# Delta rule: keys and values turned in the first stage, squares of the inversion through memory, one chunk ahead

## The chip, the cores and the metric

The kernel runs on one core of a Trainium2 chip. Its time is the device time of one execution in microseconds, the median of several runs. The core's engines are TensorE (PE, matrix products into PSUM), VectorE (DVE), ScalarE (ACT), GpSimd (POOL) and SyncE (SP, which here issues nearly all transfers). Each works through a queue of its own, in order; semaphores connect them.

## The reference

One inference step of a two-layer encoder for 2048 prompt tokens and 32 sample tokens, model width 1024, all in float32. The first layer is a gated delta rule with 8 heads of 128 channels:

```python
proj = x @ w_in                                   # q, k, v (3072 columns), z (1024), a, b (8 each)
qkv = silu(causal_conv(proj[..., :3072]))         # width 4, per channel
q = l2norm(q) * 128 ** -0.5;  k = l2norm(k)
# per head and token t, with decay g_t and strength beta_t:
#   S_t = exp(g_t) (I - beta_t k_t k_t^T) S_{t-1} + beta_t k_t v_t^T
#   o_t = S_t^T q_t
o = rmsnorm(o) * norm_w * silu(z)
x = layer_norm(alpha * x + o @ w_out)
```

It may be evaluated in blocks. With the Gram matrix of a block's keys, weighted by decay, as the strictly lower part of `tmat`, the block's updates come from solving `tmat u = v beta` and `tmat w = k beta exp(gcum)`; then the state goes from block to block. The second layer is attention over a window of two chunks with sinks, a gate and another layer norm; the change doesn't touch it.

## The kernel before, in words

Precise products are made by splitting each float32 operand into a high and a low part and adding three products (`project`, L79 to L81). The program has these stages.

**First stage** (`P1`). `w_in` has 32 row blocks of 128 channels: 8 heads of q (`i` = 0 to 7), of k (8 to 15), of v (16 to 23), then z. For each, TensorE multiplies five token blocks of 416, ScalarE copies them into a row `R` of 128 channels by all tokens, and `conv` makes the convolution and SiLU on ScalarE and VectorE: `y`, channels on partitions. `y` goes to memory by channel (scratch tensors `q`, `k`, `v`). For q and k, ScalarE squares it into the tile `th`, VectorE turns 32x32 blocks of the squares (L225) and sums over them (L226), which `norms` makes into lengths by token. From `i` = 16 on the order of work on all five engines is written out by hand (`ordered`): between the five blocks of one head stand the steps of the `conv` of the head before (a generator, advanced by `next(c)`), and the decay table E, chunk by chunk (`decays`). `th` has one buffer, `R` and `y` two.

**Gate** (`P1.z`, later `LateGate`): the products for z, 24 matmuls a block.

**Inversions ahead** (`Ahead`): beside the gate's products, the inverses of the first two chunks (the sample's 32 tokens, and the first 128 of the prompt).

**Delta stage** (`Delta`). 17 chunks: the sample's and 16 of 128 tokens. A pass `i` of the loop in `run` goes through the string `ORDER`; an entry such as `G0+2` means step G0 for chunk `i + 2`, and a digit 0 or 1 behind a name is a half of four heads. So one pass works on several chunks at different points. On TensorE, VectorE and ScalarE this order is the order of execution; SP's and POOL's queues are ordered by the planner of the language. The steps that matter:

- `Lk`, `Lq`, `Lv`, `Lz`, `LE`, `Lgb`: loads of a chunk's tiles. k has two buffers.
- `G`, `N` (L695, L702): Gram products of the keys in PSUM, times the decay table E, into the tile `npr` (two buffers).
- `NB`, `L` (L708, L717): ScalarE copies the four diagonal 32x32 blocks together, VectorE turns them so that a matrix entry stands by row and column for all heads: the squares.
- `TT`, `PC0` to `PC5`, `T1` to `T3` (`chain`, L729, L731): 31 steps of forward substitution on the squares, 25 of them (23 for the last five chunks) on POOL, the rest on VectorE.
- `SPR`, `U32`, `v1` to `v5` with the copies `y1`, `ta1`, `u1`, `ta2`, `u3`: the inverse of a 128 block out of those of 32.
- `tk`, `tv` (L818): TensorE turns k and v from channels to tokens, four heads a step; `kd`, `vn` (L825): ScalarE scales what it reads from PSUM into tiles.
- `gq`, `at`: products of keys and queries, times E. `ks`, `e`, `vp`, `vs`: what the state recalls, the error, the update. `os`, `oa`, `o`: outputs. `sp`, `SU`: the state's step.
- `sq`, `X`, `R`: norm of the outputs, with a root by Newton steps on VectorE (L484 to L495). `OSC` (L916): outputs times that root. `otr`, `z`, `st`: turned back by TensorE (L925), times the gate, stored.
- `GA0` to `GA3`, `gth`, `gz1`, `gz2`, `WH`, `WL`: the gate products still open, a quarter of a block each, with their VectorE and ScalarE steps. They end with pass 10; from pass 11 on `side` prepares the output projection.

PSUM banks of the pool `pa` (two) go to `G`, `tk`, `tv`, `gq`, v2 and v4.

After that follow the output projection, the second layer's projections and the attention.

Of the kernel before, what the change touches and what calls it, by code (L numbers as in the profile page):

```python
# [22 lines left out]
NP = 2048  # L23
# [74 lines left out]
class P1:  # L98
# [99 lines left out]
    def conv(self, i, R, parts):  # L198

        nc, T, one = self.nc, self.T, self.one  # L200
        kind, h = i // 8, i % 8
        nc.gpsimd.tensor_copy(self.convo[:, i, 0:3], R[:, NP:NP + 3])
        nc.gpsimd.tensor_copy(self.convo[:, i, 3:6], R[:, NT + 3:NT + 6])
        W = NT + 3
        y = self.big.tile([128, NT + 3], F32, tag="y", name="y")
        nc.scalar.activation(y[:], R[:, 0:W], AF.Copy, scale=self.convw[:, i, 0:1])  # L206
        for j in range(1, 4):
            yield
            nc.vector.scalar_tensor_tensor(out=y[:], in0=R[:, j:j + W], scalar=self.convw[:, i, j:j + 1], in1=y[:],  # L209
                                           op0=ALU.mult, op1=ALU.add)  # L210
# [7 lines left out]
        nc.sync.dma_start(dst[0:NTT - 1, :, h, :].rearrange("t p k -> p t k"),  # L218
                          y[:, 0:NP].rearrange("p (t k) -> p t k", k=128))
        (nc.sync if i >= self.FREE else nc.scalar).dma_start(dst[NTT - 1, :, h, 0:NS], y[:, NP + 3:NP + 3 + NS])  # L220
        if kind == 2:
            return
        nc.scalar.activation(th[:, 0:NP], y[:, 0:NP], AF.Square)
        nc.scalar.activation(th[:, NP:NT], y[:, NP + 3:NP + 3 + NS], AF.Square)
        nc.vector.transpose(R[:, 0:NT], th[:, 0:NT])  # L225
# [379 lines left out]
class Delta:  # L605
# [49 lines left out]
    def load(self, ch, name, halves=(0, 1)):  # L655
# [14 lines left out]
        else:  # L670
            for q in halves:
                if own:
                    t = ch.pool.tile([128, 4, w], F32, tag=f"c{name}{q}", name=name, bufs=1)[:]
                elif name == "q":
                    t = self.four.tile([128, 4, w], F32, tag="q", name="q", bufs=5)[:]
                else:
                    t = self.sml.tile([128, 4, w], F32, tag="vz", name=name, bufs=3)[:]
# [26 lines left out]
    def gather(self, ch):  # L704
        ch.nb = self.sml.tile([128, 8, 32], F32, tag="nb", name="nb")
        for b in range(ch.n // 32):
            bs = slice(32 * b, 32 * b + 32)
            self.nc.scalar.copy(ch.nb[bs], ch.npr[bs, :, bs])  # L708
# [5 lines left out]
    def turned(self, ch):  # L714
        n = ch.n
        ch.L = self.two.tile([128, 32, 32], F32, tag="L", name="L")
        self.nc.vector.transpose(ch.L[:n], ch.nb[:n].rearrange("q p i -> q i p").unsqueeze(2).to_broadcast([n, 32, 4, 8]))  # L717

    def chain(self, ch, P, a, z, tag):
# [6 lines left out]
        for j in range(a, z):  # L726
            i0, w = j + 1, j // 4 + 1
            sh = [n, 31 - j, w]
            P.tensor_tensor(out=tm[:n, i0 - k:, :w], in0=L[:n, i0:, j:j + 1].to_broadcast(sh),  # L729
# [85 lines left out]
    def turn(self, ch, x, name):  # L815
        tr = self.bank(self.pa, ch, name)
        for j in range(4):
            self.nc.tensor.transpose(tr[:ch.n, j, :], x[:, j, :ch.n], self.G["ident"][:, :])  # L818

    def scaled(self, ch, q, src, dst, table):  # L820
        n, tr = ch.n, ch.__dict__.pop(src + str(q))
        t = self.four.tile([128, 4, 128], F32, tag=dst, name=dst)
# [111 lines left out]
    def steps(self):  # L934
# [3 lines left out]
             "NB": self.gather, "TT": self.unit, "L": self.turned, "SPR1": self.spread, "SPR2": self.spread_back,  # L938
# [3 lines left out]
             "OSC": self.scale}  # L942
# [4 lines left out]
        for q in range(2):  # L947
# [6 lines left out]
            for name in "qvz":  # L954
                S[f"L{name}{q}"] = lambda c, name=name, q=q: self.load(c, name, (q,))
            S[f"tk{q}"] = lambda c, q=q: self.turn(c, c.k[:, self.heads(q)], f"ktr{q}")
            S[f"tv{q}"] = lambda c, q=q: self.turn(c, c.v[q], f"vtr{q}")
            S[f"kd{q}"] = lambda c, q=q: self.scaled(c, q, "ktr", "kd", "ekd")
            S[f"vn{q}"] = lambda c, q=q: self.scaled(c, q, "vtr", "vn", "hn")
# [9 lines left out]
    MADE = {"NB", "TT", "L", "T1", "T2", "T3", "PC0", "PC1", "PC2", "PC3", "PC4", "PC5"}  # L969
    HELD = {"Lgb", "Lk", "Lq0", "Lq1", "Lv0", "Lv1", "Lz0", "Lz1", "otr0", "otr1", "z0", "z1", "st0", "st1"}  # L970
    WORK = {"G0", "G1", "v1", "v2", "v3", "v4", "v5", "tk0", "tk1", "tv0", "tv1", "gq0", "gq1", "ks0", "ks1", "vp0", "vp1",
# [62 lines left out]
class Ahead(Delta):  # L1034
# [13 lines left out]
    def inverses(self, chunks):  # L1048
# [1367 lines left out]
def host_inputs(inp):  # L2416
# [116 lines left out]
```

## Time and profile before

| | |
|---|---|
| median of 3 runs | 2101.48 us (2099.33 to 2110.56) |
| profiled execution | 2110.58 us, span 2108.8 us |
| TensorE busy | 2048.6 us, 97%, granted clock 0.989 |
| VectorE, ScalarE, GpSimd busy | 1468.9 (70%), 989.0 (47%), 911.0 us (43%) |
| first stage | to about 605 us |
| inversions ahead, beside the gate | about 605 to 720 us |
| delta stage | about 720 to 1120 us |
| transferred | 360.85 MB, 171 GB/s over the span |

Rows of the timeline and of the chain that ended last start with the time from the span's start and the duration in us; then engine, line, operation and tiles. SPq rows are transfers as SP issues them. A bracket at the end of a row gives idle time before it and what released the engine. Rows of waits give the sum in us, the number of waits and the longest. TensorE's rows overlap, since matmuls are pipelined: its pace is read from start to start. A float32 product of 128x128 by 128x128 has two records, a transpose one.

### The profile page before, as it was taken

Reading aid. Unit: us, or ns where it says so; the run is one execution under the profiler, and the core shown is the slowest. Engines: PE = TensorE matmul, PEld = TensorE weight load, DVE = VectorE, ACT = ScalarE, POOL = GpSimd, SP = SyncE. Lnnn points to the kernel's source line nnn. Section 1 sums busy time; section 2 is a strip of 40 time slices with the busy share of each in tenths; the row PEclk is TensorE's granted clock in tenths of the full one; section 3 lists DMA queues with packets and bytes.
Section 4 is the critical chain, followed back from the end, with each engine's and each line's share of the span. In section 5 each row is a group of like instructions: output and inputs, shape, how many; then the busy total and the mean of one; then the engine's idle time right before and its main releaser. Section 6 shows DMA issues by size and latency. Waiting matters only on the chain.

```text
span 2108.8 us, 37301 instructions
## 1 busy us (share of the span) xinstructions
PE 2048.6 (97%) x13694; PEld 1875.4 (89%) x13694; DVE 1468.9 (70%) x2587; ACT 989.0 (47%) x2465; POOL 911.0 (43%) x1248
## 2 busy tenths in 40 slices
PE   7999999999999999999999999999999999999998
PEld 5999999999999999999887887889989997777775
DVE  4476666675647678888887887768877755566565
ACT  4354444446532267777762211534644445455552
POOL 0322223212222177778752112157436515566666
PEclk9999999999999999999999999999999999999999
DMA  5132333236665545455766666778776659533421
GB/s 206 33 90 88 97 110 111 82 102 226 193 185 179 182 137 179 159 169 182 271 209 227 212 213 219 254 229 296 243 240 222 226 171 317 127 101 107 114 72 66
DMA packets 292763, 360.85 MB, mean 171 GB/s; under 512 B 74260, under 2 KB 217460, under 8 KB 292564
## 3 DMA queue, kind: packets, MB, share of 16 engines
q1 hardware_dynamic: 278576, 334.29, 49.9%
q10 hardware_dynamic: 14004, 24.17, 3.6%
q8 instruction: 108, 1.77, 0.3%
q14 instruction: 75, 0.61, 0.1%
HBM read 235.54 MB, written 134.06 MB: 175 GB/s over the span
## 4 chain that ended last, share of the span: by engine, by line
PE 83%; DMA 7%; DVE 3%; POOL 3%; issue 2%; ACT 1%; SPq 0%; ACTq 0%; DVEq 0%; POOLq 0%
PE ps L79 12%; PE ps L81 11%; PE ps L80 11%; PE ot L1126 3%; PE ot L1127 3%; PE ot L1128 3%; PE S L1992 2%; PE po L1126 2%; PE ot L2025 2%; PE po L1128 2%; PE po L1127 2%; PE tr L2007 2%; PE X L1653 2%; PE X L1651 2%; PE X L1652 2%
## 5 line engine op out<-in xcount | busy, mean ns | idle before, releaser
L79 PE MATMUL ps<-act_hi,w_hi 128*128 128x416 f32 x1280 | 454.9, 355 | 0.0
L81 PE MATMUL ps<-act_hi,w_lo 128*128 128x416 f32 x1280 | 450.2, 352 | 0.0
L80 PE MATMUL ps<-act_lo,w_hi 128*128 128x416 f32 x1280 | 447.9, 350 | 0.0
L79 PEld LDWEIGHTS ps<-act_hi,w_hi 128*128 128x128 f32 x1280 | 240.3, 188 | 3.8 <-issue 0.4
L80 PEld LDWEIGHTS ps<-act_lo,w_hi 128*128 128x128 f32 x1280 | 240.6, 188 | 3.0
L81 PEld LDWEIGHTS ps<-act_hi,w_lo 128*128 128x128 f32 x1280 | 240.1, 188 | 3.3
L209 DVE SCALAR_TENSOR_TENSOR y<-R,convw,y 128x2083 f32<-128x2083 f32 x72 | 182.5, 2536 | 60.9 <-ACT y L206 44.9
L56 POOL TENSOR_TENSOR w_lo<-w_raw,w_hi 128x1024 fp32r<-128x1024 f32 x25 | 71.4, 2858 | 330.9 <-ACT w_hi L55 303.6
L729 POOL TENSOR_TENSOR tm<-L,Tt 128x60 f32<-128x60 f32 (+19 forms) x365 | 132.5, 363 | 84.8 <-issue 39.9
L1826 POOL TENSOR_TENSOR P<-e,sm 128x384 f32<-128x384 f32 (+2 forms) x128 | 102.3, 820 | 118.0 <-DVE sm L1816 111.6
L731 POOL TENSOR_TENSOR Tt<-Tt,tm 128x60 f32<-128x60 f32 (+19 forms) x365 | 139.8, 383 | 28.6
L1812 ACT ACTIVATE e<-S,nm 128x193 f32<-128x193 f32 (+2 forms) x260 | 104.6, 415 | 97.3 <-DVE nm L1807 56.5
L1330 DVE TENSOR_TENSOR w_lo<-w_raw,w_hi 128x512 fp32r<-128x512 f32 x132 | 136.7, 1053 | 18.5 <-ACT w_hi L1342 12.7
L1126 PE MATMUL po<-wo_hi,g_hi 128*128 128x512 f32 x256 | 104.9, 410 | 8.1 <-DVE r L1134 7.9
L305 ACT COPY R<-ps 128x416 f32<-128x416 f32 (+1 forms) x144 | 60.4, 442 | 109.3 <-PE ps L81 95.8
L1482 ACT ACTIVATE o<-X 128x416 f32<-128x416 f32 x80 | 41.4, 518 | 134.7 <-PE X L1653 134.6
L1126 PE MATMUL ot<-wo,g_hi 128*128 128x512 f32 x256 | 103.6, 405 | 0.0
L1128 PE MATMUL po<-wo_hi,g_lo 128*128 128x512 f32 x256 | 101.2, 396 | 0.5 <-DVE g_lo L1169 0.5
L1127 PE MATMUL po<-wo_lo,g_hi 128*128 128x512 f32 x256 | 101.1, 395 | 0.0
L1127 PE MATMUL ot<-wo,g_hi 128*128 128x512 f32 x256 | 100.8, 394 | 0.0
L1128 PE MATMUL ot<-wo,g_lo 128*128 128x512 f32 x256 | 100.8, 394 | 0.0
L1342 ACT CAST w_hi<-w_raw 128x512 fp32r<-128x512 f32 x129 | 76.8, 616 | 21.5 <-PE ps L1652 6.7
(362 smaller groups left out, 5119.4 us busy)
## 6 DMA issues: line engine op xcount, KB each, us to landing
w_raw<-in_b_w SPq DMA_DIRECT2D x60, 512.0 KB
w_raw<-in_w_in SPq DMA_DIRECT2D x40, 512.0 KB
act_raw<-s_hT SPq DMA_DIRECT2D x64, 208.0 KB
s_rows<-o SPq DMA_DIRECT2D x50, 208.0 KB
k<-s_k SPq DMA_DIRECT2D x17, 512.0 KB
E<-s_E SPq DMA_DIRECT2D x17, 512.0 KB
s_bq<-s_rows SPq DMA_DIRECT2D x40, 208.0 KB
s_bz<-o SPq DMA_DIRECT2D x40, 208.0 KB
```

Of the source, the lines that this page charges most:

```text
L79: nc.tensor.matmul(ps, hi[:, k, :], xh[:, k, :], start=(k == 0), stop=False)
L80: nc.tensor.matmul(ps, hi[:, k, :], xl[:, k, :], start=False, stop=False)
L81: nc.tensor.matmul(ps, lo[:, k, :], xh[:, k, :], start=False, stop=(k == KC - 1))
L209: nc.vector.scalar_tensor_tensor(out=y[:], in0=R[:, j:j + W], scalar=self.convw[:, i, j:j + 1], in1=y[:], op0=ALU.mult, op1=ALU.add)
L729: P.tensor_tensor(out=tm[:n, i0 - k:, :w], in0=L[:n, i0:, j:j + 1].to_broadcast(sh), in1=Tt[:n, j:j + 1, :w].to_broadcast(sh), op=ALU.mult)
L731: P.tensor_tensor(out=Tt[:n, i0:, :w], in0=Tt[:n, i0:, :w], in1=tm[:n, i0 - k:, :w], op=ALU.subtract)
L1126: nc.tensor.matmul(ps[:n], ghi[:, k, :n], hi, start=a, stop=False)
L1127: nc.tensor.matmul(ps[:n], ghi[:, k, :n], lo, start=False, stop=False)
L1128: nc.tensor.matmul(ps[:n], glo[:, k, :n], hi, start=False, stop=z)
L1330: P.tensor_tensor(out=lo, in0=raw, in1=hi, op=ALU.subtract)
L1812: self.nc.scalar.activation(x.e[:, h, u, :x.n], x.S[:, h, u, :], AF.Exp, bias=x.nm[:, h, u:u + 1], scale=1.0, accum_out=x.sm[:, h, u:u + 1])
L1826: self.nc.gpsimd.tensor_tensor(out=x.P[:, u, :nj * 128].rearrange("r (j h k) -> r j h k", h=2, k=64), in0=x.e[:, :, u, :n].rearrange("r h ...
```

## The change

Keys and values are turned to token order in the first stage and go to memory that way; k still goes by channel as well, and by token into the new scratch tensor `kt`. VectorE turns 32x32 blocks of `y` into `th`, and four pairs of transfers write 32 channels each: pieces of 32 floats, every 4 KB. For k, ScalarE squares the turned tile into `R`, and VectorE sums. In the delta stage one load of 512 KB each (`Lt`, `Lv`) brings kd and vn by token, and ScalarE scales them in place; the steps `tk` and `tv` are gone. The squares go from `npr` to memory (`WN`, four transfers of 32x32 blocks of all heads), and come back as four loads that read each head's square on the partitions that use it (`L`); `NB` and the VectorE transpose are gone, and `chain` reads the square by the other index. `G` and `N` are made one chunk earlier, at the end of a pass, and `Lk` stands in the middle.

```diff
@@ conv
-        dst = T["qkv"[kind]]
-        nc.sync.dma_start(...)                      # by channel, for q, k and v
-        if kind == 2:
-            return
-        nc.scalar.activation(th[:, 0:NP], y[:, 0:NP], AF.Square)
-        nc.vector.transpose(R[:, 0:NT], th[:, 0:NT])
+        if kind < 2:
+            dst = T["qk"[kind]]
+            nc.sync.dma_start(...)                  # by channel, for q and k
+        pieces = (th[:, 0:NP], y[:, 0:NP]), (th[:, NP:NT], y[:, NP + 3:NP + 3 + NS])
+        if kind == 0:
+            for a, b in pieces:
+                nc.scalar.activation(a, b, AF.Square)
+            nc.vector.transpose(R[:, 0:NT], th[:, 0:NT])
+        else:
+            for a, b in pieces:
+                nc.vector.transpose(a, b)
+            self.by_token(T[("kt", "v")[kind - 1]], h, th)
+            if kind == 2:
+                return
+            yield
+            nc.scalar.activation(R[:, 0:NT], th[:, 0:NT], AF.Square)
+    def by_token(self, dst, h, turned):
+        for a in range(4):
+            s = slice(32 * a, 32 * a + 32)
+            self.nc.sync.dma_start(dst[0:NTT - 1, :, h, s].rearrange("t (b i) j -> i (t b) j", i=32),
+                                   turned[s, 0:NP].rearrange("i (b j) -> i b j", j=32))
+            self.nc.sync.dma_start(dst[NTT - 1, 0:NS, h, s], turned[s, NP:NT])
@@ ordered
-                for _ in range((2, 2, 1, 1, 0)[b]):
+                for _ in range((2, 2, 1, 1, int(i == self.FREE + 1))[b]):
@@ Delta
     ORDER = """
-        ta2+0 fq1+1 os0+0 v5+0 Lk+2 PC2+1 OSC+-1 Lq1+2 PC3+1 fq0+1 vn0+1 G0+2 u3+0 N0+2 G1+2 TT+2 otr0+-1
-        otr1+-1 N1+2 GA1+1 z0+-1 NB+2 tk0+1 tk1+1 vp0+0 vs0+0 PC4+1 kd0+1 st0+-1 z1+-1 Lv1+1 GA3+0 fk+1 L+2
-        PC5+1 kd1+1 vp1+0 Lv0+2 st1+-1 T1+1 oa0+0 T2+1 sp0+0 T3+1 tv1+1 SPR1+1 PC0+2 LE+3 o0+0 vs1+0 SU0+0 gq1+2
-        PC1+2 SPR2+1 os1+0 sp1+0 vn1+1 Lz0+0 oa1+0 SU1+0 sq0+0 at1+2 v1+1 Lgb+2 WH+1 gq0+2 at0+2 o1+0 y1+1 ks0+1
-        e0+1 U32+1 ks1+1 v2+1 v3+1 GA2+1 gth+0 sq1+0 WL+1 X+0 Lz1+0 Lq0+3 ta1+1 v4+1 gz1+0 tv0+2 GA0+2 u1+1 e1+1
-        R+0 gz2+0
+        ta2+0 fq1+1 os0+0 v5+0 PC2+1 OSC+-1 Lq1+2 PC3+1 L+2 fq0+1 vn0+1 u3+0 TT+2 otr0+-1 otr1+-1
+        GA1+1 z0+-1 vp0+0 vs0+0 PC4+1 kd0+1 st0+-1 z1+-1 GA3+0 fk+1 PC5+1 kd1+1 vp1+0 st1+-1 T1+1
+        oa0+0 T2+1 sp0+0 T3+1 SPR1+1 PC0+2 LE+3 o0+0 vs1+0 SU0+0 gq1+2 PC1+2 SPR2+1 os1+0 sp1+0
+        vn1+1 Lz0+0 oa1+0 SU1+0 sq0+0 at1+2 v1+1 Lgb+2 Lt+2 WH+1 gq0+2 at0+2 o1+0 y1+1 ks0+1
+        e0+1 U32+1 ks1+1 Lk+3 v2+1 v3+1 GA2+1 gth+0 sq1+0 Lv+2 WL+1 X+0 Lz1+0 Lq0+3 ta1+1
+        v4+1 G0+3 gz1+0 GA0+2 u1+1 N0+3 G1+3 e1+1 R+0 N1+3 WN+3 gz2+0
+    def by_token(self, ch, src, dst):
+        t = self.two.tile([128, 8, 128], F32, tag=dst, name=dst)
+        ch.__dict__[dst] = t[:, 0:4], t[:, 4:8]
+        self.nc.sync.dma_start(t[:ch.n], self.T[src][ch.ti, :ch.n])
-    def gather(self, ch):
-        ch.nb = self.sml.tile([128, 8, 32], F32, tag="nb", name="nb")
+    def keep_squares(self, ch):
         for b in range(ch.n // 32):
             bs = slice(32 * b, 32 * b + 32)
-            self.nc.scalar.copy(ch.nb[bs], ch.npr[bs, :, bs])
+            self.nc.sync.dma_start(self.T["N"][ch.ti, b].rearrange("p j i -> j p i"), ch.npr[bs, :, bs])
-    def turned(self, ch):
+    def squares_back(self, ch):
         ch.L = self.two.tile([128, 32, 32], F32, tag="L", name="L")
-        self.nc.vector.transpose(ch.L[:n], ch.nb[:n].rearrange("q p i -> q i p").unsqueeze(2).to_broadcast([n, 32, 4, 8]))
+        for b in range(ch.n // 32):
+            src = self.T["N"][ch.ti, b].rearrange("p j i -> p (j i)").unsqueeze(0).to_broadcast([4, 8, 1024])
+            self.nc.sync.dma_start(ch.L[32 * b:32 * b + 32].rearrange("q j i -> q (j i)"), src)
@@ chain
-            P.tensor_tensor(out=tm[:n, i0 - k:, :w], in0=L[:n, i0:, j:j + 1].to_broadcast(sh),
+            P.tensor_tensor(out=tm[:n, i0 - k:, :w], in0=L[:n, j, i0:].unsqueeze(2).to_broadcast(sh),
@@ scaled: no tiles of its own, no PSUM
+        n, t = ch.n, ch.__dict__[name][q]
         for j in range(4):
             h = q * 4 + j
+            self.nc.scalar.activation(t[:n, j, :], t[:n, j, :], AF.Copy, scale=self.G[table][:n, ch.ti, h:h + 1])
@@ inverses (Ahead)
-            self.gather(tmp)
+            self.keep_squares(tmp)
             self.unit(tmp)
             yield
-            self.turned(tmp)
+            self.squares_back(tmp)
@@ SCRATCH
+    "kt": (NTT, 128, 8, 128),
+    "N": (NTT, 4, 8, 32, 32),
```

More of the change, by code (lines that the diff above doesn't have):

```diff
@@ L216, in conv @@
         yield
-        dst = T["qkv"[kind]]
-        nc.sync.dma_start(dst[0:NTT - 1, :, h, :].rearrange("t p k -> p t k"),
-                          y[:, 0:NP].rearrange("p (t k) -> p t k", k=128))
-        (nc.sync if i >= self.FREE else nc.scalar).dma_start(dst[NTT - 1, :, h, 0:NS], y[:, NP + 3:NP + 3 + NS])
-        if kind == 2:
-            return
-        nc.scalar.activation(th[:, 0:NP], y[:, 0:NP], AF.Square)
-        nc.scalar.activation(th[:, NP:NT], y[:, NP + 3:NP + 3 + NS], AF.Square)
-        nc.vector.transpose(R[:, 0:NT], th[:, 0:NT])
+        if kind < 2:
+            dst = T["qk"[kind]]
+            nc.sync.dma_start(dst[0:NTT - 1, :, h, :].rearrange("t p k -> p t k"),
+                              y[:, 0:NP].rearrange("p (t k) -> p t k", k=128))
+            (nc.sync if i >= self.FREE else nc.scalar).dma_start(dst[NTT - 1, :, h, 0:NS], y[:, NP + 3:NP + 3 + NS])
+        pieces = (th[:, 0:NP], y[:, 0:NP]), (th[:, NP:NT], y[:, NP + 3:NP + 3 + NS])
[11 more added lines that the diff above has]
+            nc.scalar.activation(R[:, 0:NT], th[:, 0:NT], AF.Square)
         nc.vector.tensor_reduce(out=parts[:, h, :], in_=R[:, 0:NT].rearrange("p (c j) -> p c j", j=32),
@@ L676, in load @@
                 else:
-                    t = self.sml.tile([128, 4, w], F32, tag="vz", name=name, bufs=3)[:]
+                    t = self.sml.tile([128, 4, w], F32, tag="z", name=name, bufs=3)[:]
                 ch.__dict__.setdefault(name, {})[q] = t
                 nc.sync.dma_start(t[:, :, :n], T[name][ti, :, q * 4:q * 4 + 4, :n])
+    def by_token(self, ch, src, dst):
+        t = self.two.tile([128, 8, 128], F32, tag=dst, name=dst)
+        ch.__dict__[dst] = t[:, 0:4], t[:, 4:8]
+        self.nc.sync.dma_start(t[:ch.n], self.T[src][ch.ti, :ch.n])
     @staticmethod
@@ L813, in join5_out, with scaled @@
             self.nc.scalar.mul(self.u[:64, ps, 64:128], ch.u2p[hv, ps], -1.0)
[L815 to L822, printed above, removed]
+    def scaled(self, ch, q, name, table):
+        n, t = ch.n, ch.__dict__[name][q]
         for j in range(4):
             h = q * 4 + j
-            self.nc.scalar.activation(t[:n, j, :], tr[:n, j, :], AF.Copy, scale=self.G[table][:n, ch.ti, h:h + 1])
-        ch.__dict__.setdefault(dst, {})[q] = t
+            self.nc.scalar.activation(t[:n, j, :], t[:n, j, :], AF.Copy, scale=self.G[table][:n, ch.ti, h:h + 1])
     def pairs(self, ch, q):
@@ L941, in steps @@
              "u3": self.join5_out, "fk": lambda c: self.fade(c, c.k, slice(0, 8)), "X": self.mean, "R": self.root,
-             "OSC": self.scale}
+             "OSC": self.scale, "Lt": lambda c: self.by_token(c, "kt", "kd"), "Lv": lambda c: self.by_token(c, "v", "vn")}
         for j in range(6):
@@ L953, in steps @@
                 S[f"{name}{q}"] = lambda c, f=f, q=q: f(c, q)
-            for name in "qvz":
+            for name in "qz":
                 S[f"L{name}{q}"] = lambda c, name=name, q=q: self.load(c, name, (q,))
[L956 to L959, printed above, removed]
+            S[f"kd{q}"] = lambda c, q=q: self.scaled(c, q, "kd", "ekd")
+            S[f"vn{q}"] = lambda c, q=q: self.scaled(c, q, "vn", "hn")
             S[f"fq{q}"] = lambda c, q=q: self.fade(c, c.q[q], self.heads(q))
@@ L968 @@
     INVERT = {"v1", "y1", "v2", "ta1", "v3", "u1", "v4", "ta2", "v5", "u3", "U32", "G0", "G1", "N0", "N1"}
-    MADE = {"NB", "TT", "L", "T1", "T2", "T3", "PC0", "PC1", "PC2", "PC3", "PC4", "PC5"}
-    HELD = {"Lgb", "Lk", "Lq0", "Lq1", "Lv0", "Lv1", "Lz0", "Lz1", "otr0", "otr1", "z0", "z1", "st0", "st1"}
-    WORK = {"G0", "G1", "v1", "v2", "v3", "v4", "v5", "tk0", "tk1", "tv0", "tv1", "gq0", "gq1", "ks0", "ks1", "vp0", "vp1",
+    MADE = {"WN", "TT", "L", "T1", "T2", "T3", "PC0", "PC1", "PC2", "PC3", "PC4", "PC5"}
+    HELD = {"Lgb", "Lk", "Lq0", "Lq1", "Lz0", "Lz1", "otr0", "otr1", "z0", "z1", "st0", "st1"}
+    WORK = {"G0", "G1", "v1", "v2", "v3", "v4", "v5", "gq0", "gq1", "ks0", "ks1", "vp0", "vp1",
             "os0", "os1", "oa0", "oa1", "sp0", "sp1", "otr0", "otr1"}
@@ L1057, in inverses @@
         yield
-        for name in ("gb", "q", "v"):
+        for name in ("gb", "q"):
             self.load(chunks[0], name)
```

3 lines of the change are left out of this document (1 added, 2 removed).

## The prediction

> **What bounds the kernel now.** I read the page's first table, then the stretches by time, the waits of the delta stage, and last the timelines of TensorE (PE) and VectorE (DVE) through one of its iterations.
>
> ```profile
> span 2108.8 us, 37301 instructions
> PE 2048.6 (97%) x13694; PEld 1875.4 (89%) x13694; DVE 1468.9 (70%) x2587; ACT 989.0 (47%) x2465; POOL 911.0 (43%) x1248
> ```
>
> ```profile
> core 0: us, PE busy (x) PEld busy (x) DVE busy (x) ACT busy (x) POOL busy (x), PEclk, DMA share, GB/s
> 500.00:550.00 50.00, 50.00 (x267) 49.54 (x266) 30.02 (x22) 32.22 (x71) 15.33 (x13) 1.00 0.71 221
> 760.00:860.00 100.00, 100.00 (x1137) 95.98 (x1136) 85.68 (x204) 70.59 (x227) 78.73 (x205) 1.00 0.50 163
> ```
>
> TensorE is full in the first stage (500 to 550 us) and in the delta stage (760 to 860), at full granted clock. In the delta stage each chunk of 128 tokens is one pass through `ORDER`, and the start of its Gram products G shows the pace in the chain that ended last:
>
> ```profile
> 761.97 1.98 PE g L695 x16
> 784.88 1.98 PE g L695 x16
> 951.39 1.98 PE g L695 x16
> ```
>
> From 784.88 to 951.39 are seven passes: 23.79 us each. The waits between 760 and 960 have no row for TensorE. POOL, which carries 25 of the 31 steps of each inversion, waits little:
>
> ```profile
> POOL tm L729 <- DVE tm L729: 12.0, 9, 1.6
> ```
>
> That is 1.33 us a pass: its own pace is 23.79 - 1.33 = 22.46. So two engines stand near the limit, and TensorE is a hair ahead. One pass on TensorE (start, duration):
>
> ```profile
> 856.17 2.05 PE L695 MATMUL g<-k 128*128 128x128 f32 x16
> 858.06 1.04 PE L925 MATMUL otr<-ident,o 128*128 128x128 f32 x8
> 860.07 1.03 PE L818 MATMUL ktr<-ident,k 128*128 128x128 f32 x8
> ...
> 865.64 0.60 PE L818 MATMUL vtr<-ident,v 128*128 128x128 f32 x4
> 866.97 1.06 PE L870 MATMUL op<-Sp,q 128*128 128x128 f32 x8
> 871.37 1.95 PE L846 MATMUL ks<-Sp,k 128*128 128x128 f32 x16
> 873.25 0.62 PE L779 MATMUL tp<-y,u 64*64 64x64 f32 x13
> ...
> 876.73 0.66 PE L818 MATMUL vtr<-ident,v 128*128 128x128 f32 x4
> 878.36 1.05 PE L870 MATMUL op<-Sp,q 128*128 128x128 f32 x8
> 879.35 0.68 PE L808 MATMUL u2p<-u,ta 64*64 64x64 f32 x16
> 879.96 0.38 PE L695 MATMUL g<-k 128*128 128x128 f32 x1
> ```
>
> and on VectorE, up to the multiplication OSC (L916) whose result `otr` turns back:
>
> ```profile
> 874.55 0.68 DVE L854 TENSOR_TENSOR vn<-vn,ks 128x512 f32<-128x512 f32 x1
> 875.14 0.17 DVE L484 TENSOR_SCALAR ro_y<-Xo 128x8 int32<-128x8 int32 x1
> ...
> 877.39 0.77 DVE L563 SCALAR_TENSOR_TENSOR z<-zth,z 128x416 f32<-128x416 f32 x1
> 878.09 0.82 DVE L841 TENSOR_TENSOR q<-q,gb 128x512 f32<-128x512 f32 x1
> 878.82 1.37 DVE L916 TENSOR_TENSOR o<-o,ro_y 128x1024 f32<-128x1024 f32 x1
> ```
>
> Both engines run their program order here: the rows follow `ORDER` step by step.
>
> **The change part by part.** *Transposes off TensorE.* Sixteen a chunk go (tk, tv). Sixteen products of G take 1.89 us by starts (856.17 to 858.06), and a transpose is one such record, so at most 0.12 each: 8 ktr and 4 vtr within the stretch 858.06 to 873.25 are 1.3 (taken as 0.87 + 0.44), all sixteen 1.74 us a pass, 17 chunks at most 30 us. This is worth that much only while TensorE sets the pace.
>
> *Turned writes in the first stage.* VectorE gets 8 large transposes for v; those for k take the place of the ones of the squares:
>
> ```profile
> L225 DVE STREAM_TRANSPOSE R<-th 128x2080 f32<-128x2080 f32 x16 | 37.5, 2341 | 37.8 <-ACT th L224 37.8
> L717 DVE STREAM_TRANSPOSE L<-nb 128x1024 f32<-128x1024 f32 (+1 forms) x17 | 34.4, 2022 | 1.7 <-ACT nb L708 1.7
> ```
>
> 8 x 2.34 = 19 us, under a TensorE that needs 120 matmuls x 50/267 = 22.5 us a head; in 500 to 550 VectorE is 60% busy and would be 70%. Cost 0; without that cover 19 us. SP gets eight issues a head in place of two for v, beside two for k. A megabyte of 512-byte rows holds SP as long as the short transfer behind it is stuck in its issue (min/median/max):
>
> ```profile
> L220 SPq DMA_DIRECT2D s_v<-y x8: 1596/3185/5999, 455.1 to 604.3; - x8
> ```
>
> The same megabyte in 128-byte pieces costs between the same 3.2 us (price by bytes) and 4 x 3.2 = 12.8 (by pieces). I take the middle, 8, since these writes are short pieces in many rows: behind them queue the weight fetch, the decay table's loads and the gate's stores, and the `th` tile stays taken. Both ends lie under 22.5 us, and six PSUM buffers let TensorE run on: 0, at either end.
>
> *Squares through memory.* Seventeen L717 (2.02 us) leave VectorE, and the copies of the diagonal blocks leave ScalarE; both engines had slack, so 0 in themselves. In their place come four small stores, a wait on them, and four loads a chunk on SP. kt adds 512 KB a chunk, the squares as much again; DMA was at 0.50.
>
> *Gram products one chunk ahead, at the end of a pass.* This is the part that decides. `G0+3` now stands behind v4, `N0+3` behind `gz1`, and ahead of `e1`, the root R and OSC on VectorE. That adds a wait: VectorE's N0 waits for G0, and behind N0 are queued e1, R, N1, gz2, fq1, OSC; TensorE's otr waits for OSC, and the rest of TensorE's pass waits behind otr. G0 itself waits for the k tile, whose buffer (two of them) comes free with `ks1` of the same pass. So a ring closes once a pass:
>
> N0 starts 0.92 after G0 (the rows below), then N0 0.69, e1 0.59 (874.55 to 875.14), R 2.25 (875.14 to 877.39), N1 0.69, gz2 0.70 and fq1 0.73 (to the next start each), OSC 1.37: 7.9, with the signal 8.0.
>
> ```profile
> 723.33 1.78 PE g L695 x16
> ```
>
> ```profile
> 724.25 0.69 DVE L702 TENSOR_TENSOR npr<-g,E 128x512 f32<-128x512 f32 x1 [0.79 <-PE g L695]
> ```
>
> otr to the end of ks1 on TensorE: 873.25 - 858.06 = 15.19, less the 1.3 of transposes: 13.9. Then the wait for k, at least the work in front of G0 (873.25 to 876.73: 3.48). The k loads after the gate's products have ended show their price, from the chain and from SP's issue to TensorE's start:
>
> ```profile
> 1011.67 6.43 DMA k<-s_k
> 1035.22 5.44 DMA k<-s_k
> ```
>
> ```profile
> 990.12 0.32 SPq L666 DMA_DIRECT2D k<-s_k  x1
> 1056.20 0.32 SPq L666 DMA_DIRECT2D k<-s_k  x1
> ```
>
> ```profile
> 994.75 1.46 PE L695 MATMUL g<-k 128*128 128x128 f32 x11 [0.36 <-DMA k<-s_k]
> 1060.39 2.05 PE L695 MATMUL g<-k 128*128 128x128 f32 x16
> ```
>
> 4.63, 6.43, 5.44, and at most 4.19 (no wait): mean 5.2, which I take; ends 3.48 and 6.43. Today G starts 6.7 us after ks1, so this load is hidden; that cover goes. A pass becomes 8.0 + 13.9 + 5.2 = 27.1 us against 23.79. Even with k at no cost it is 25.4: without the ring's wait TensorE would reach otr 0.95 (G0, half of 1.89) + 1.2 (GA0, 876.73 to 878.36 less four transposes) + 0.95 (G1) + 0.99 (os0, 878.36 to 879.35) + 0.61 (v5, to 879.96) = 4.7 us after G0's start, and OSC ends 8.0 after it.
>
> *Sum.* G of chunk 3 to G of chunk 16 (761.97 to 1060.39) is 298.4 us in 13 passes. After: nine full ones, 243.9; one without a gate product after otr (1.2 less), 25.9; one without two, 24.6; two without gz2 as well, 23.9 each: 342.2, or +44. Before chunk 3, three chunks lose their transposes (-5), while each of the two inversions done ahead waits for its squares (two landings, some 6 us; the second is in VectorE's way): 0 together. After chunk 16 there is no G left to wait for, and the squares' round trip stands in front of the last inversion: 0 to +5, taken as 0. So +44 on the profiled 2110.58, which is 2155; that run was 9 us above the median of the three, 2101.48, and on the median the sum is 2145.
>
> **The rivals.** *Faster: the late start of R does not reach TensorE.* Then the pace falls to POOL's 22.46: 9 x 1.33, and 4 x 1.74 where POOL has fewer steps: -19, 2082. It decides if OSC ends within 4.7 us of G0, 3.3 earlier than the rows say. For it speaks that VectorE loses 2.02 us a pass; against it, that none of the lost work lies between G0 and OSC. 12%.
>
> *k hidden.* If k lands within 3.48, passes are 25.4, 24.2, 22.9 and 22.2: 320, +22, 2123. For it: 4.19 at the most once. Against: the three others, and 1 MB more to move a pass. 12%.
>
> *The squares land late and POOL sets the pace.* N1 ends 5.1 after G0; four issues at 0.4 and a small store as below, four issues and a load like k's: they land 5.1 + 1.6 + 3.3 + 1.6 + 5.2 = 16.8 after G0.
>
> ```profile
> 994.92 3.31 DMA s_z<-z
> ```
>
> POOL then needs 22.46, the rest of the steps to ks1 some 7 to 9, k 5.2, in two passes: 25.7 to 26.7 each, just under the 27.1. Five us more in the loads give 28.2 to 29.2, some +1.6 x 11 on top: 2163. 8%. [...]
>
> *The token writes slow the first stage.* Should a 128-byte piece cost twice a 512-byte row, a head holds the queue 25.6 us against 22.5: 16 x 3.1, +50 on top, 2195. 5%. [...]
>
> **How the numbers follow.** The three runs span 0.53% of their median, so 0.5% (10.5 us) is about what tells from no change. The forecast has 63%: 2130 to 2163 by the ends of k. 2108 to 2172 takes in k hidden and the late squares, with 6 us either side for what the start and the tail hold: 83%. Faster 0.12; slower is the rest but for 0.07 in which k is hidden and the tail gains.
>
> **What would show it.** Right: G to G near 27 us; waits of G on `k<-s_k` and of otr on DVE o L916, some 1.7 and 3.3 us a pass; no PE wait before 600; POOL waiting several us a pass. Wrong: a gapless TensorE in the delta stage, G to G under 23.8, or PE waits in the first stage.

## The result, and the profile after

| | before | after |
|---|---|---|
| median (4 runs each, the same chip) | 2105.18 us (2099.33 to 2110.56) | 2237.14 us (2234.03 to 2240.17) |
| ratio, 95% interval | | 1.0628 (1.0605 to 1.0651) |
| profiled span | 2108.8 us | 2231.9 us |
| TensorE's granted clock | 0.989 | 0.96 |

The change makes the kernel 6.3% slower. The forecast was slower by 2%: the direction and the ring that it named hold, the size doesn't. The profiled executions are 123.1 us apart and the medians 132.0, since the profile before is of the slowest of its four runs and the one after of the fastest. The page of the changed kernel, first table:

```profile
span 2231.9 us, 37147 instructions
PE 2060.5 (92%) x13422; PEld 1888.1 (85%) x13422; DVE 1448.8 (65%) x2594; ACT 970.5 (43%) x2392; POOL 878.7 (39%) x1248
```

TensorE has fewer instructions and is busy for longer: some of them run slower, which the stretches by time explain (PEclk is the granted clock of the stretch):

```profile
core 0: us, PE busy (x) PEld busy (x) DVE busy (x) ACT busy (x) POOL busy (x), PEclk, DMA share, GB/s
425.00:450.00 25.00, 11.71 (x56) 11.22 (x56) 19.69 (x9) 8.81 (x10) 8.10 (x8) 0.73 0.60 129
700.00:750.00 50.00, 42.04 (x202) 39.88 (x201) 28.70 (x85) 9.87 (x19) 6.84 (x15) 0.86 0.66 203
760.00:860.00 100.00, 87.82 (x856) 82.05 (x856) 60.84 (x158) 52.78 (x169) 55.28 (x150) 0.90 0.55 167
```

The stretch 760 to 860 was full at clock 1.00 before. There are also holes at 425 to 450 (first stage) and 700 to 750 (start of the delta stage) that I had priced at nothing. The Gram products G mark the passes again, those of chunks 3, 12 and 16 in TensorE's timeline:

```profile
785.28 0.91 PE L718 MATMUL g<-k 128*128 128x128 f32 x6 [1.25 <-DMA k<-s_k]
1053.46 0.77 PE L718 MATMUL g<-k 128*128 128x128 f32 x2 [3.76 <-DMA k<-s_k]
1182.01 1.41 PE L718 MATMUL g<-k 128*128 128x128 f32 x5 [8.20 <-DMA k<-s_k]
```

Before, they started at 761.97, 973.97 and 1060.39 (the second one in its timeline:)

```profile
973.97 0.38 PE L695 MATMUL g<-k 128*128 128x128 f32 x1
```

So the 123.1 us of longer span divide like this:

| stretch | before | after | longer by | forecast |
|---|---|---|---|---|
| up to G of chunk 3 | 762.0 | 785.3 | 23.3 | 0 |
| nine passes to G of chunk 12 | 212.0 | 268.2 | 56.2 | 31.9 |
| four passes to G of chunk 16 | 86.4 | 128.6 | 42.1 | 11.9 |
| from there to the end | 1048.4 | 1049.9 | 1.5 | 0 |

Waits of TensorE between 780 and 1185, and one pass on TensorE:

```profile
PE g L718 <- DMA k<-s_k: 57.7, 13, 9.1
PE otr L945 <- DVE o L936: 26.8, 11, 3.4
```

```profile
872.48 2.05 PE L718 MATMUL g<-k 128*128 128x128 f32 x8 [3.47 <-DMA k<-s_k]
...
874.67 0.55 PE L80 MATMUL ps<-act_lo,w_hi 128*128 128x416 f32 x1
875.02 0.55 PE L81 MATMUL ps<-act_hi,w_lo 128*128 128x416 f32 x1
...
877.99 1.06 PE L890 MATMUL op<-Sp,q 128*128 128x128 f32 x8
...
881.47 1.94 PE L945 MATMUL otr<-ident,o 128*128 128x128 f32 x8 [1.81 <-DVE o L936]
...
883.55 0.55 PE L80 MATMUL ps<-act_lo,w_hi 128*128 128x416 f32 x1
883.90 0.55 PE L81 MATMUL ps<-act_hi,w_lo 128*128 128x416 f32 x1
...
886.10 0.35 PE L80 MATMUL ps<-act_lo,w_hi 128*128 128x416 f32 x1
886.28 0.35 PE L81 MATMUL ps<-act_hi,w_lo 128*128 128x416 f32 x1
...
902.80 1.13 PE L718 MATMUL g<-k 128*128 128x128 f32 x8 [2.36 <-DMA k<-s_k]
...
903.96 0.35 PE L80 MATMUL ps<-act_lo,w_hi 128*128 128x416 f32 x1
904.15 0.35 PE L81 MATMUL ps<-act_hi,w_lo 128*128 128x416 f32 x1
```

The two waits of the ring are there, once a pass each. What the forecast lacked is beside them: after the first two of these waits a matmul of 416 columns starts every 0.35 us (874.67 to 875.02, and 883.55 to 883.90), later in the pass every 0.19 (886.10 to 886.28). Not every wait does this: after the 2.36 us before 902.80 the pace is 0.19 at once (903.96 to 904.15). The kernel before, with no wait, ran its passes from 760 to 860 at a granted clock of 1.00.

The granted clock is 0.50 from 872.50 to 877.00, behind the wait of 3.47 us, and from 881.50 to 884.20, behind that of 1.81, and 1.00 from 884.90 to 890.00; behind the wait of 2.36 us it is 1.00 from 902.80 to 906.00. So behind some of the waits TensorE runs at half clock. Behind 881.47 the pace is back at 0.19 from 884.83 on: 3.4 us at half clock, of which half, 1.7 us, is an estimate of the loss. r3 below agrees with it: TensorE's work outside its one wait is 23.7 us in six of nine passes and 22.1 in one, a step of 1.6. The 1.81 us before 881.47 were enough, although the speed had been full again at 877.99 (eight matmuls in 1.06 us, against 1.94 at 881.47). What decides which waits cost the clock stays open.

### The profile page after: what moved, and what is told of

Read it like the earlier page. It is cut to its first block, busy times and chain, and to the rows that moved or that the text cites. A ratio compares the mean times of both kernels' runs of the same rounds, so it can differ in the third digit from the quotient of the medians.

```text
span 2231.9 us, 37147 instructions
## 1 busy us (share of the span) xinstructions
PE 2060.5 (92%) x13422; PEld 1888.1 (85%) x13422; DVE 1448.8 (65%) x2594; ACT 970.5 (43%) x2392; POOL 878.7 (39%) x1248
## 3 DMA queue, kind: packets, MB, share of 16 engines
q8 instruction: 106, 1.74, 0.3%
## 4 chain that ended last, share of the span: by engine, by line
PE 69%; DMA 13%; DVE 9%; POOL 3%; issue 3%; SPq 2%; ACT 1%; DVEq 0%; ACTq 0%; POOLq 0%
PE ps L79 8%; PE ps L81 8%; PE ps L80 8%; DMA k<-s_k 4%; PE ot L1144 3%; PE ot L1145 3%; PE ot L1146 3%; PE X L1671 2%; PE X L1669 2%; PE X L1670 2%; PE S L2010 2%; PE po L1144 2%; PE po L1146 2%; PE po L1145 2%; PE tr L2025 2%
## 5 line engine op out<-in xcount | busy, mean ns | idle before, releaser
L79 PE MATMUL ps<-act_hi,w_hi 128*128 128x416 f32 x1280 | 462.1, 361 | 8.0 <-DVE z L576 5.2
L81 PE MATMUL ps<-act_hi,w_lo 128*128 128x416 f32 x1280 | 455.6, 356 | 0.0
L80 PE MATMUL ps<-act_lo,w_hi 128*128 128x416 f32 x1280 | 454.2, 355 | 0.0
L79 PEld LDWEIGHTS ps<-act_hi,w_hi 128*128 128x128 f32 x1280 | 244.9, 191 | 13.4 <-DVE z L576 5.9
L81 PEld LDWEIGHTS ps<-act_hi,w_lo 128*128 128x128 f32 x1280 | 244.7, 191 | 3.8
L756 POOL TENSOR_TENSOR tm<-L,Tt 128x60 f32<-128x60 f32 (+19 forms) x365 | 117.2, 321 | 223.2 <-DMA L<-s_N 169.1
L56 POOL TENSOR_TENSOR w_lo<-w_raw,w_hi 128x1024 fp32r<-128x1024 f32 x25 | 62.1, 2482 | 303.2 <-ACT w_hi L55 277.9
L1348 DVE TENSOR_TENSOR w_lo<-w_raw,w_hi 128x512 fp32r<-128x512 f32 x132 | 136.3, 1049 | 15.5 <-ACT w_hi L1360 11.3
L758 POOL TENSOR_TENSOR Tt<-Tt,tm 128x60 f32<-128x60 f32 (+19 forms) x365 | 134.2, 368 | 28.6
L718 PE MATMUL g<-k 128*128 128x128 f32 (+1 forms) x288 | 51.8, 345 | 59.0 <-DMA k<-s_k 59.0
L718 PEld LDWEIGHTS g<-k 128*128 128x128 f32 (+1 forms) x288 | 49.0, 255 | 61.4 <-issue 59.4
```

The costliest lines, as they stand in the source:

```text
L79: nc.tensor.matmul(ps, hi[:, k, :], xh[:, k, :], start=(k == 0), stop=False)
L80: nc.tensor.matmul(ps, hi[:, k, :], xl[:, k, :], start=False, stop=False)
L81: nc.tensor.matmul(ps, lo[:, k, :], xh[:, k, :], start=False, stop=(k == KC - 1))
L756: P.tensor_tensor(out=tm[:n, i0 - k:, :w], in0=L[:n, j, i0:].unsqueeze(2).to_broadcast(sh), in1=Tt[:n, j:j + 1, :w].to_broadcast(sh), op=A ...
L758: P.tensor_tensor(out=Tt[:n, i0:, :w], in0=Tt[:n, i0:, :w], in1=tm[:n, i0 - k:, :w], op=ALU.subtract)
L1348: P.tensor_tensor(out=lo, in0=raw, in1=hi, op=ALU.subtract)
```

## The experiments

Each is timed beside the kernel before on one chip; ratios are to that. "Changed" stands for the changed kernel, 1.0628.

**r1: the hole in the first stage.** The chain of the changed kernel up to the product that waits 13.3 us (`n_ps` on `parts`):

```profile
386.69 1.96 ACT th L213
388.67 2.34 DVE y L215
391.09 2.32 DVE th L229
393.86 2.95 SPq L248
400.43 2.80 DMA s_kt<-th
403.41 3.40 DMA wo_parts<-in_a_w_out
...
409.13 2.68 DMA s_wo<-wo_parts
411.91 1.96 ACT th L213
...
444.09 2.19 PE n_ps L480 x8
```

A ring, that is a chain of steps whose first waits for the last of the round before, runs through the one buffer of `th` and takes 25.2 us a head (386.69 to 411.91). The parts of the output weights borrow that buffer (`wo_parts`) between two heads. Once `th` is turned (393.41), the writes to kt hold it for 9.8 us, and TensorE needs 22.5 us a head.

```diff
+            turned = R if kind == 1 else th
-                nc.vector.transpose(a, b)                          # into th
+                nc.vector.transpose(turned[:, c], b)
-            nc.scalar.activation(R[:, 0:NT], th[:, 0:NT], AF.Square)
+            nc.scalar.activation(th[:, 0:NT], R[:, 0:NT], AF.Square)
```

> Only the first stage is changed: the turned keys stand in the row tile R (two buffers), the squares in th, so th is no longer held by the writes to kt. Theory: the 13.3 us wait of the norms' product in the first stage comes from a ring of 25.2 us a head through the one buffer th (tanh, product, turn, writes to kt, then the load, split and store of an output weight in the same buffer) against 22.5 us of matmuls; with R the ring is shorter than 22.5, the wait is gone, and the time falls by 13 us to about 2224. Rival: the short writes themselves are too slow for the queue; the wait stays, 2237.

Measured 2227.9 us, 1.0581 (1.0557 to 1.0604). The wait is 4.6 us in place of 13.3, so 9 of 13 us are gone. The ring was the cause, and it isn't fully open: the weights' load stands in SP's queue behind the writes.

**r8: the rest of that hole.**

```diff
-            if 6 <= i < self.FREE:
+            if i < self.FREE - 6:
                 next(self.wo)
```

> The changed kernel with one edit in the first stage: the parts of the output weights, which borrow the tile th, are made beside the heads of q and the first of k (i = 0 to 8) instead of beside i = 6 to 14. Theory: the heads of k then hold th only for tanh, product, turn and their own writes, some 17 us against 22.5 us of matmuls; the 13.3 us wait of the norms' product goes altogether (r1, which left the weights there, kept 4.6): 13 to 14 us less, about 2223. Rival: the short writes fill the queue by themselves, a wait of 4 us or more stays: 2228 or more.

Measured 2232.0 us, 1.0620 (1.0584 to 1.0655), where 2223 was expected. The wait on `parts` is gone altogether, with the 128-byte writes as they are, so their price alone is below 22.5 us a head. But the edit has its own price at the start of the kernel, where ScalarE waits for the first part's store and TensorE behind it (waits of TensorE to 450 us):

```profile
PE ps L79 <- ACT R L323: 5.5, 1, 5.5
```

**r2: root first.** `e1+1 R+0` and `OSC` moved ahead of `gz1+0`, and so ahead of N0 on VectorE:

```diff
-        v4+1 G0+3 gz1+0 GA0+2 u1+1 N0+3 G1+3 e1+1 R+0 N1+3 WN+3 gz2+0       (OSC+-1 in the next pass)
+        v4+1 G0+3 e1+1 R+0 OSC+0 gz1+0 GA0+2 u1+1 N0+3 G1+3 N1+3 WN+3 gz2+0
```

> Only VectorE's order in the delta stage: e1, the root R and OSC stand ahead of N0. Theory (the ring G, N0, root, OSC, otr): the wait of otr on OSC (2.4 us a pass) ends, G to otr falls from 8.6 to about 4.7 us, the wait for k stays; a pass goes from 30.1 to about 25.6, and the time falls by some 55 us to about 2180 (2170 to 2195). Rival (squares that land late and GpSimd behind them set the pace): passes stay above 29 us, time above 2225.

Measured 2236.9 us, 1.0617 (1.0590 to 1.0644): nothing. Not by the rival's reason, though. TensorE and SP in one pass:

```profile
898.87 2.05 PE L717 MATMUL g<-k 128*128 128x128 f32 x8 [5.34 <-DMA k<-s_k]
...
902.79 1.50 PE L717 MATMUL g<-k 128*128 128x128 f32 x8
...
906.67 1.09 PE L944 MATMUL otr<-ident,o 128*128 128x128 f32 x8 [0.87 <-ACT u L839]
...
929.26 2.05 PE L717 MATMUL g<-k 128*128 128x128 f32 x8 [5.11 <-DMA k<-s_k]
```

```profile
918.32 1.73 SPq L696 DMA_DIRECT2D z<-s_z  x2
...
920.62 0.38 SPq L701 DMA_DIRECT2D kd<-s_kt  x1
921.09 0.38 SPq L686 DMA_DIRECT2D E<-s_E  x1
921.52 0.42 SPq L683 DMA_DIRECT2D k<-s_k  x1
```

The wait on OSC has ended, and G waits 5 us for k in place of 3: G starts 7.7 us after the issue of k, at the end of a burst of z, q, kd and E. After that longer wait G itself runs at half clock, 3.92 us from G0 to G1, where G0 and the six gate matmuls behind it take 2.1 at full clock (902.80 to 904.90 in the changed kernel). So G to otr is still 7.8 us. One wait went, the other took its place and the clock went with it.

**r3: no wait for k.** The step G takes the key tile of the chunk before (`chunks[c - 1].k`), so its products are those of another chunk; the load of k stays.

> G of chunk c takes the keys of chunk c - 1, which have long been there, so G doesn't wait for the load; the Gram products are those of another chunk. Theory: the wait for k (3.5 us a full pass, 5 to 9 in the last four) ends; ring 8.0 + 14.0 + 3.5 = 25.5 us a pass, with some loss of clock 26; the time falls by some 55 to 65 us to about 2177. Rival (squares and GpSimd): passes stay above 28 us, time above 2215.

Measured 2179.4 us, 1.0350 (1.0323 to 1.0377): 58 us less, as expected. G to G is 27.0 us in most passes; the wait of otr on OSC is the one left in each of them (waits of TensorE, 780 to 1130). One such wait left the clock alone (the second row, with matmuls at full speed behind it):

```profile
PE otr L945 <- DVE o L936: 30.9, 9, 4.4
```

```profile
926.00 1.06 PE L945 MATMUL otr<-ident,o 128*128 128x128 f32 x8 [3.34 <-DVE o L936]
```

**r5 and r9: all the rings open.** r5 joins r2 with a third buffer for k:

```diff
-    BUFS = 2
+    BUFS = 3                      # Lk+3 stands early in the pass, issued by nc.scalar; z has 2 buffers
-        self.nc.scalar.copy(ch.Tt[:ch.n], self.tinit[:ch.n])
+        self.nc.sync.dma_start(ch.Tt[:ch.n], self.I["tinit"][:ch.n])
```

r9 adds:

```diff
-            ... activation(ch.vn[q][:n, j, :], ch.o[:n, h, :], AF.Square, accum_out=...)
+            ... activation(ch.vs[q][:n, j, :], ch.o[:n, h, :], AF.Square, accum_out=...)
-        ... sq1+0 Lv+2 ...
+        ... vp1+0 Lv+2 ...        # and the load to Tt by nc.scalar
```

> VectorE's order as in r2 (e1, root and OSC ahead of N0) and a third buffer for k, whose load is issued on ScalarE's queue early in the pass (room for it: two z buffers in place of three, the unit tile loaded straight to Tt). Theory: a pass has two rings, root to otr and k to G, and each alone only hands its wait to the other; with both open a pass is 22.05 us of matmuls or GpSimd's own 22.46, with a few late squares 22.5 to 23.5, matmuls run at the full clock, and the time falls by some 100 us to about 2137 (2125 to 2150). Rival (the squares' way through memory and GpSimd behind it set the pace once the rings are open): passes of 25.7 to 29, 2165 to 2200.

> r5 with the third ring opened: the squares of the outputs no longer use vn as their scratch tile but vs, so vn is free after vp1, and Lv stands there; the unit tile's load goes by ScalarE's queue. Theory: in r5 ScalarE waited 42 us for vn, which lands 6 to 9 us after its late issue, and u3 and so otr stood behind it; with that open and GpSimd no longer behind it a pass is 22.5 to 24 us, about 2140 (2130 to 2155). Rival: squares that land late (GpSimd waited 34 us for them in r5) are what makes the passes long: 26 us or more a pass, 2165 or more.

Measured 2181.2 us, 1.0353 (1.0330 to 1.0376), and 2185.4, 1.0384 (1.0367 to 1.0402). They are 56 and 52 us better than the changed kernel and about 45 short of what I expected: the rival holds. In r9 TensorE no longer waits for k or OSC but for the inversions (35.9 us in nine waits, 780 to 1120), and GpSimd waits for squares (its waits, 780 to 1120, and one place in its timeline, with TensorE's G and SP's issues of the same squares):

```profile
POOL tm L754 <- DMA L<-s_N: 38.1, 7, 7.6
```

```profile
880.34 0.25 POOL L754 TENSOR_TENSOR tm<-L,Tt 128x31 f32<-128x31 f32 x1 [7.14 <-DMA L<-s_N]
933.08 0.25 POOL L754 TENSOR_TENSOR tm<-L,Tt 128x31 f32<-128x31 f32 x1 [7.31 <-DMA L<-s_N]
```

```profile
916.95 0.38 PE L716 MATMUL g<-k 128*128 128x128 f32 x1
```

```profile
920.89 1.80 SPq L730 DMA_DIRECT2D s_N<-npr  x4
...
924.28 2.79 SPq L742 DMA_DIRECT2D L<-s_N  x4
```

The squares are used 16.1 us after G (916.95 to 933.08), and two inversions take 52.7 us from wait to wait (880.34 to 933.08): twice GpSimd's 22.46 and one wait. That is 26.4 us a pass; TensorE alternates between 23.0 and 28 to 31. The forecast's estimate for this rival, 16.8 us to land and 25.7 to 26.7 a pass, is what a pass comes to once the rings are out of the way, but its sum fits in part by luck: it held 5.2 us for k in two passes, and r9 has no wait for k. In place of k stand VectorE's part of the inversion and the half clock behind the wait for it (ks at 962.04 takes 3.28 us, where the changed kernel at full clock takes 1.95): from GpSimd's last step (ends 955.79) to the next G (968.73) are 12.9 us, where the forecast had 7 to 9 and k. The five us more in the loads, which the forecast's 2163 holds, aren't in these rows: 16.1 us from G to use, against 16.8 without them.

**r4 and r12: squares on chip.** r4 makes all of them as before (`NB+3` in the place of `WN+3`), r12 only those of the two inversions done ahead.

> Squares gathered by ScalarE and turned by VectorE as in the kernel before; everything else as in the changed kernel, G one chunk ahead at the end of a pass. Theory: passes keep their 29.8 us, since the ring and the wait for k set them; what goes is the start of the delta stage, where two inversions wait for their squares and hold VectorE's queue while the gate's products wait behind them (14.5 us between 700 and 750) and one late square at 800 (3.4 us and the clock behind it): -16 to -20, about 2219. Rival (late squares set the pace of the passes): passes fall to 26 or below, time about 2165.

> The changed kernel, but the two inversions done ahead gather and turn their squares on chip as before; the passes are the changed kernel's. Theory: the gate's products between 700 and 750 wait for VectorE, which stands with the second inversion behind squares that land 6.4 us after their issue and behind the steps that this delays; three waits of 2.8, 2.5 and 2.7 us and the half-speed matmuls behind them, 14.5 in all, go: 2223 (2220 to 2227). Rival: those waits come from the late products of the first stage or the transfers of z: 2232 or more.

r4 measured 2241.7 us, 1.0637 (1.0610 to 1.0665). It doesn't tell what it was made for: `NB` on ScalarE waits for N1 there, with ta2 and u3 behind it, and TensorE waits for those instead (between 780 and 1180). Only its start speaks: G of chunk 3 comes at 772.2 in place of 785.3. The wait:

```profile
PE u2p L830 <- ACT ta L825: 26.4, 12, 3.2
```

r12 measured 2226.1 us, 1.0566 (1.0540 to 1.0592), 11 us less. In the profiles 11.5 us go before G of chunk 3 (773.8 in place of 785.3), and 5.9 come back behind it. Its stretch from 700 to 750:

```profile
700.00:750.00 50.00, 47.53 (x282) 46.16 (x281) 35.35 (x92) 14.58 (x34) 7.30 (x15) 1.00 0.70 220
```

So the second hole was the squares' trip of the two inversions done ahead (r12 doesn't separate the two): VectorE stands in its chain, and the gate's products wait for VectorE to empty their banks.

**r7: the waits filled.**

```diff
+    def warm(self, ps, m):
+        for j in range(m):
+            self.nc.tensor.matmul(ps[:, j % 4, :], self.G["ident"][:, :], self.G["ident"][:, :], start=True, stop=True)
```

> The changed kernel with matmuls of the identity into the bank that is about to be written, 12 ahead of G0 (2.8 us) and 8 ahead of otr (1.9 us), which fill most of two waits of TensorE a pass and are overwritten. Theory (granted clock): the matmuls that follow a wait take 0.35 us in place of 0.19 until the clock is back, 1.7 us a pass; kept busy, TensorE keeps the clock, otr to the end of ks1 falls from 14.7 to 14.0 and G to otr from 8.6 to 8.0, and the time falls by some 15 to 20 us to about 2220 though work is added. Rival: the slow matmuls come from something else, such as transfers into the same memory: no change, or up to 10 us more by the fillings that overrun the wait.

Measured 2232.8 us, 1.0611 (1.0595 to 1.0627): within the intervals, no change. The clock is as expected (nine passes of r7, then of the changed kernel):

```profile
781.69:1044.91 263.22, 243.36 (x2643) 231.82 (x2642) 160.14 (x433) 139.77 (x453) 164.24 (x457) 0.99 0.54 174
```

```profile
785.28:1053.46 268.18, 219.07 (x2297) 209.20 (x2297) 160.10 (x433) 139.85 (x453) 161.71 (x459) 0.90 0.55 173
```

The clock is back at 0.99, and a pass is 29.25 us in place of 29.80. From chunk 4 to 12 the two parts outside k's wait fall to 8.04 us (G to otr) and 14.00 (otr to the end of ks1), 1.2 less together, as expected; from there to G it is 7.24 in place of 6.81, so k takes back 0.4. The span as a whole is only 0.9 us shorter, since the stretch behind G of chunk 16 is 7.5 longer, for which no row here gives the reason. That the clock follows the waits is shown, and 1.2 us a pass of it; a gain in time is not.

**r11: one load fewer ahead of k.**

> The changed kernel without the loads of kt from chunk 4 on: kd stays the tile of an earlier chunk, scaled by 1, so ScalarE's work is the same and 512 KB a pass fewer are loaded. Open: why ks1's end to G took 6.9 us a pass and not the 5.2 of the kernel before. Theory (a burst): k is issued behind kd and E and shares the transfer engines with them; without kd it lands 1 to 2 us sooner, ks1 to G falls from 6.9 to about 5.3, and the time falls by some 15 to 25 us to about 2217. Rival: k's own price after its buffer comes free; ks1 to G stays near 6.9, time 2230 or more.

Measured 2227.6 us, 1.0577 (1.0555 to 1.0599), between the two. ks1's end to G is 6.2 us in place of 6.8 (means over the passes from chunk 4 to 12), yet its profiled span is only 3.4 us shorter: 5.0 before chunk 3 and 4.9 in the four last passes, less 3.1 by which the nine passes are longer (271.3 against 268.2) and 3.4 behind them. How much of k's time in flight is contention stays open.

**r6, r10 and r13: keys and values by token alone.** The kernel before without tk and tv, kd and vn loaded by token and scaled in place, squares on chip, G and N at the start of a pass as they were. r6 has r1's edit; r10 adds r8's and r9's (scratch vs, Lv early); r13 differs from r10 by:

```diff
-            if i < self.FREE - 6:
+            if 1 <= i < 10:
                 next(self.wo)
-    SPLIT = 25, 23
+    SPLIT = 24, 22
```

> The kernel before with keys and values by token alone: no tk and tv on TensorE, squares gathered and turned on chip, G and N where they were at the start of a pass; in the first stage the turned keys stand in R as in r1. Theory: that part of the change is good; TensorE needs 22.05 us a pass, GpSimd 22.46, k stays hidden, the first stage pays nothing: 17 to 20 us below the kernel before, about 2088 (2082 to 2095). Rival: one megabyte more a pass and the loads of kd and vn in SP's queue push k or E late, or the short writes slow the first stage: 2105 or more.

> r6 (the kernel before with keys and values by token) with the ring through vn opened as in r9 and the output weights early as in r8. Theory: r6 lost 6.6 us before chunk 3 (3 of them the wait of the norms' product) and its passes stood at 23.2 by the load of vn, which ScalarE waits for ahead of u3 and otr; now GpSimd's 22.46 sets a pass and the first stage pays nothing: 2104 less 13 to 18, about 2088, the only version below the kernel before. Rival: the transposes on TensorE were hidden by GpSimd anyway or another load comes late: 2100 or more.

> r10 with two more edits: the output weights beside i = 1 to 9 (at i = 0 they held ScalarE for 14.7 us and TensorE for 5.5), and one step of each inversion moved from GpSimd to VectorE (24 and 22 in place of 25 and 23). Theory: the 5.5 us go, and GpSimd's pace falls from 22.5 to about 21.7, below TensorE's 22.1: 2101 less 5.5 less 13 x 0.5, about 2090, 0.7% below the kernel before. Rival: VectorE's longer part of the inversion, on the same chain to v1, gives the step back: 2095 to 2100.

r6 measured 2113.7 us, 1.0046 (1.0030 to 1.0062): the rival's time, by another load than the k or E that it named. Its nine passes take 207.5 us, 4.5 fewer than before, but G of chunk 3 comes 6.5 later (768.50). The passes stay above GpSimd's 22.46 because the loads by token bring a ring of their own: the squares of the outputs use vn as scratch to the end of a pass, so that vn's load comes late and ScalarE waits for it (its waits, 780 to 1070):

```profile
ACT vn L843 <- DMA vn<-s_v: 31.3, 13, 3.3
```

r10 measured 2101.5 us (2086.9 to 2106.4 over ten runs), 0.9977 (0.9954 to 0.9999). Passes came to GpSimd's 22.5 as expected, but the early weights' 5.5 us were in it. r13 measured 2084.9 us, 0.9903 (0.9885 to 0.9920): 1.0% below the kernel before. From G of chunk 3 to that of chunk 12 TensorE is full, at full clock:

```profile
757.25:955.16 197.91, 196.96 (x2294) 188.52 (x2290) 182.78 (x460) 154.07 (x488) 162.76 (x434) 1.00 0.60 200
```

Seven passes of it, each 22.09 us:

```profile
779.54 0.71 PE L719 MATMUL g<-k 128*128 128x128 f32 x4 [0.30 <-DMA k<-s_k]
934.15 1.05 PE L719 MATMUL g<-k 128*128 128x128 f32 x7
```

That is 23.79 less the 1.74 that the forecast gave for sixteen transposes, within 0.04 us.

## Why the prediction was wrong

**The bound and the transposes: right.** TensorE gapless at 23.79 us with GpSimd at 22.46 behind it; sixteen transposes worth 1.74 us only while TensorE sets the pace. r10 and r13 show both numbers: without the transposes r10's pass is 22.5, GpSimd's pace, and r13's, with a step of each inversion less on GpSimd, 22.09.

**The ring: right in kind, two of three terms off.** In passes without half-speed matmuls the changed kernel shows G to otr 7.95 (8.0 taken) and otr to the end of ks1 13.98 (13.9 taken). Over the eight passes from chunk 4 to 12 the means are 8.55 and 14.70, and 6.81 from ks1 to G where 5.2 was taken: 30.05 us in place of 27.1. Of the 2.95 missing, 1.6 are k's and 1.3 the clock's: with the clock back in r7, the other two terms measure 8.04 and 14.00, as forecast. For the load of k I averaged four values, one of them no duration but an upper bound of a load that made no one wait, and took none of the added traffic into it. How much of the 1.6 that traffic explains stays open (r11). The granted clock was not in the sum, though the forecast itself brought TensorE two waits a pass.

**The last four passes: wrong.** They were given 23.9 to 25.9 us, as if work that leaves TensorE shortened the ring by as much, and measured 30.5 to 35.6. From otr to the end of ks1 the last two are only 0.8 us shorter than a full pass, and from ks1 to G the four take 7.3 to 11.3 us, where 5.2 was taken. k takes longer there, beside the loads of the output weights (512 KB each, issued at 1165.87 and 1170.12; G's row of 1182.01 is above):

```profile
1172.47 0.32 SPq L684 DMA_DIRECT2D k<-s_k  x1
```

That is 9.5 us from its issue to G. r3, without that wait, gives 101.8 us for the four in place of 128.6.

**First stage at 0: wrong, 13.5 of the 23.3 us** (the wait of 13.3 and the half clock behind it, 0.50 from 446.00 to 447.40, less what TensorE was ahead). The step compared the writes with 22.5 us a head, and r8 bears that out. What it left out is who else uses their tile: I wrote that "the th tile stays taken" and didn't ask who takes it next. The rows of `wo_parts` name that tile's second user.

**Start of the delta stage at 0: wrong, about 10 us.** "Two landings, some 6 us; the second is in VectorE's way" was the right place. The 6 us were set off against transposes that TensorE no longer makes, when it was waiting; and behind VectorE stood three waits of TensorE, 8.0 us together, and the half clock after them (0.50 from 722 to 727, behind the first).

**The rivals.** k hidden (2123): r3 is that case, at 2179, since clock, start and first stage were missing from all cases alike. Squares late (2163): there, under the rings, with the size forecast. No run shows the five us more in the loads that 2163 is worked out from; in their place r9 shows 26.4 us a pass, within the 25.7 to 26.7 of the sum without them. Faster (2082): the reason given against it holds; r13 comes near that time (2085) by leaving two of the three parts out. Token writes (2195): no run shows a 128-byte piece at twice the price of a 512-byte row, on which it rested; r8 shows the writes below 22.5 us a head, where that price would be 25.6. The range missed because its ends moved terms inside the passes, and 0 for the stretches outside had 6 us of room.

## What to carry to other kernels

When a step is moved so that a ring closes, list all the rings before pricing one: here k and OSC each held a pass at 27 us or more, the squares one at 26.4 behind them, and opening a single one moved the time by 0 (r2) or by 58 us (r3). A wait added to TensorE can cost more than itself: in r3 half clock took 1.6 us behind it in six of nine passes, so put that into the sum. And where a transfer holds a tile for longer, look up every other user of that tile's buffer, not only the engine that writes it next.

## What the runs showed of the hardware that I had not expected

TensorE's matmuls fell to half clock (0.50 granted; 0.35 us in place of 0.19) after a wait as short as 1.81 us, for some 3 us there and some 5 after the wait of 3.47. The length of a wait alone doesn't decide it: after 2.36 us (902.80 in the changed kernel) and 3.34 us (926.00 in r3) they kept full speed. In r7 waits filled with matmuls kept the clock at 0.99.
